# HGRN2 recurrence on one core: three short-column visits per head instead of four, and one projection operand re-read from DRAM

## The chip, the cores and the metric

The kernel runs on one core of one Trainium2 chip. The metric is device time in microseconds (us); the time of before is the median of three runs. One more execution was taken with the hardware profiler; its own time and span stand in the table further down.

## The reference, cut to what matters

A two-layer network over 1024 tokens of width 1024: layer 0 is sliding-window attention, layer 1 the HGRN2 recurrence; each is followed by a squared-ReLU MLP. The change touches layer 1 alone. There, eight heads of width 128 work in 16 chunks of 64 tokens:

```python
q, f, i, g = jnp.split(h @ w_in, 4, axis=-1)
...
def chunk_step(state, inp):
    qc, kc, vc, lc = inp                       # lc: log of the forget gate
    b = jnp.cumsum(lc, axis=2)
    o_inter = jnp.einsum('bhtd,bhde->bhte', qc * jnp.exp(b), state)
    diff = b[:, :, :, None, :] - b[:, :, None, :, :]
    decay = jnp.exp(jnp.where(causal[None, None, :, :, None], diff, -jnp.inf))
    scores = jnp.einsum('bhtd,bhtsd,bhsd->bhts', qc, decay, kc)
    o_intra = jnp.einsum('bhts,bhse->bhte', scores, vc)
    ...
```

`scores` is a 64 x 64 causal table per chunk whose entry (t, s) carries the product of all forget gates between s and t, for each of the 128 channels.

## The kernel before, in words

**The input projection.** `hgrn` runs eight heads. For each, `gates` calls `two` twice (q with g, then f with i). `two` multiplies by a seven-product scheme (Strassen-Winograd): the activations were prepared as seven operands `x[1]` to `x[7]`, each four tiles that are held as a rounded high part and a low part, in the buffer pool `a` (60 buffers of 256 KB). One product is 12 matmuls of 128x128 by 512 columns: high weights by high and by low activations, low weights (`wl`) by high activations. Each product goes to a PSUM bank of pool `p` and is read from there into a tile of pool `t` (18 buffers) by a copy on ScalarE or an addition on VectorE.

**The recurrence.** `recurrence` builds `scores` level by level. Level lg pairs neighbouring blocks of 2^lg tokens: the later block's queries meet the earlier block's keys. Between levels `double` multiplies the changed half of q and of k by the block products of the forget gates, so that after `double(H)` blocks of 2H tokens are joined. The score matmuls have 64 output rows each and are issued in pairs, one for each half of the array ("columns" in the code, `128*64` in the profile); all other matmuls use the whole array (`128*128`). A stretch of score matmuls between whole-array ones is called a *visit* here. Before, each head has four: diagonal (`own`) with level 0; levels 1 and 2; levels 3 and 4; level 5 with `cross`. `double(1)`, `double(4)` and `double(16)` write in place; `double(2)`, `double(8)` and `double(32)` write new tiles (their unchanged half is copied by ScalarE), because the two levels of a visit need the values before and after it. `late` lists every operand of a visit as an input of each of its matmuls, so no matmul of it starts before all are ready. `merge` puts a level's results into `scores` on VectorE (a predicated copy).

**The order.** All operations are recorded first, then a planner with a table of costs puts them in order on each engine and gives each tile its buffer; the kernel issues that order. `interleave` records the recurrence of head e-1 between the projection steps of head e, so the visits of a head stand among products of the next. Every operation is recorded by one helper, so all carry line 433 in the profile, and groups are told apart by tile names: `q<-t,t` in form `128*64` are the visits, `p<-a,wh` and `p<-a,wl` the projection. DMAs are all issued on SyncE's queue (SP), which takes them in order.

**Moving data to DRAM and back** is done by `put_by` (stores the two parts of an operand) and `take_back` (loads them into buffers of pool `a`).

Of the kernel before, what the change touches and what calls it, by code (L numbers as in the profile page):

```python
# [378 lines left out]
class Net:  # L379
# [1051 lines left out]
    def take_back(self, kept):  # L1431
# [2 lines left out]
            self.dma(v.bitcast(F32), k, 4 * P * TH)  # L1434
        return views

    def two_first(self, which, e, x):

        self.s.lead = LEAD
        w = [self.weight_split(self.raw(self.io["win"][which[0], e][:, c : c + TH])) for c in (0, TH)]  # L1440
        self.s.lead = 0
        main, own, y0 = self.psum(), self.psum(), self.t()
        self.product(main, w[0], x[1], True)
        self.copy(y0, main)
        self.product(own, w[1], x[2], True)
        self.tt("DVE", y0, own, y0, ALU.add)
        return main, y0

    def two(self, which, e, x, out, begun=None):

        w = self.strassen_weights(*(self.io["win"][i, e] for i in which), (1, 2) if begun else ())
        main, y0 = begun or (self.psum(), self.t())
        side, own = self.psum(), begun or self.psum()
        y1, z0, z1 = (self.t() for _ in range(3))
        out += [(y0, y1), (z0, z1)]
        if not begun:
            self.product(main, w[1], x[1], True)
            self.copy(y0, main)
        yield
        self.product(side, w[5], x[5], True)  # L1460
        self.copy(z1, side)
        yield
        self.product(main, w[6], x[6], False)
        self.copy(y1, main)
        yield
        if not begun:
            self.product(own, w[2], x[2], True)
            self.tt("DVE", y0, own, y0, ALU.add)
        yield
        self.product(main, w[7], x[7], False)  # L1470
        self.tt("DVE", z1, main, z1, ALU.add)
        yield
        self.product(side, w[3], x[3], False)
        self.tt("DVE", y1, side, y1, ALU.add)
        yield
        self.product(main, w[4], x[4], False)
        self.copy(z0, main)
        yield
# [31 lines left out]
    def recurrence(self, e, gates, totals, out):  # L1510

        nc = self.nc
        NC = NH * BPH
        chunk = lambda z, j: z[:, j * CH : j * CH + CH]
        scores = self.t(F32, (P, NC, CH))
        tots, tot = [self.t(tag="m") for _ in range(NH)], [g[1] for g in gates]
        qs, ks = ([g[i] for g in gates] for i in (0, 2))
        later = lambda z, H: z.rearrange("p (n a h) -> p n a h", a=2, h=H)[:, :, 1]
        at = 0

        def level(lg, part, qs, ks, late):
            H = 1 << lg
            for hf, (q, k) in enumerate(zip(qs, ks)):
                for c in range(BPH):
                    for b in range(2):
                        rows, j = slice(b * CH, b * CH + CH), 2 * c + b
                        self.mm(part[rows, hf * BPH + c], chunk(k, j), later(chunk(q, j), H), True, True, CH, 2.06, "columns", late)

        def merge(lg, part):
            H = 1 << lg  # L1530
            n = CH // (2 * H)
            mask = later(self.level_mask[lg], H).unsqueeze(1).to_broadcast([P, NC, n, H])
            target = scores.rearrange("p c (n a h) -> p c n a h", a=2, h=H)[:, :, :, 1]
            part = part.rearrange("p c (n h) -> p c n h", n=n)
            self.op("DVE", nc.vector.copy_predicated, [target], [mask, part], 70 + TH // 2 * 1.04, target, mask, part)

        def part_of(bank, i):
            return bank[:, i * TH // 2 : (i + 1) * TH // 2].rearrange("p (c t) -> p c t", c=NC)

        own = self.psum("q").rearrange("p (c t) -> p c t", c=NC)  # L1540
        part = part_of(self.psum("q"), 0)
        first = [self.t() for _ in range(NH)]
        for z, (q, f, k, g, v) in zip(first, gates):
            self.tt("any", z, q, f, ALU.mult)
        late = qs + ks + first
        for hf, (q, k) in enumerate(zip(qs, ks)):
            for c in range(BPH):
                for b in range(2):
                    rows, j = slice(b * CH, b * CH + CH), 2 * c + b
                    self.mm(own[rows, hf * BPH + c], chunk(k, j), chunk(q, j), True, True, CH, 2.06, "columns", late)  # L1550
        level(0, part, first, ks, late)
        self.tt("DVE", scores, own, self.diag.unsqueeze(1).to_broadcast([P, NC, CH]), ALU.mult)
        merge(0, part)
        qs = first
        yield
        at, tot, qs, ks = self.double(1, qs, ks, tot, tots, at)
        yield
        for lg in (1, 3, 5):
            bank = self.psum("q")
            at, tot, q2, k2 = self.double(1 << lg, qs, ks, tot, tots, at, True)  # L1560
            yield
            late = qs + ks + q2 + k2
            level(lg, part_of(bank, 0), qs, ks, late)
            if lg < LEVELS - 1:
                level(lg + 1, part_of(bank, 1), q2, k2, late)
            else:
                cross = self.psum("q")[:CH].rearrange("p (c t) -> p c t", c=NC)
                for hf, (q, k) in enumerate(zip(q2, k2)):
                    for c in range(BPH):
                        self.mm(cross[:, hf * BPH + c], chunk(k, 2 * c), chunk(q, 2 * c + 1), True, True, CH, 3.9, "columns", late)  # L1570
            merge(lg, part_of(bank, 0))
            qs, ks = q2, k2
            if lg < LEVELS - 1:
                merge(lg + 1, part_of(bank, 1))
                yield
                at, tot, qs, ks = self.double(2 << lg, qs, ks, tot, tots, at)
            yield
        weights = []
        for hf in range(NH):
            s, c = self.t(F32, (P, BPH, 2, CH)), slice(hf * BPH, hf * BPH + BPH)  # L1580
# [5 lines left out]
        at, tot, qs, ks = self.double(CH, qs, ks, tot, tots, at)  # L1586
# [4 lines left out]
        for hf, (q, k) in enumerate(zip(qs, ks)):  # L1591
# [13 lines left out]
            before = [state]  # L1605
# [26 lines left out]
        self.dma(z, kept, 4 * P * TH)  # L1632
        return z

    def double(self, H, qs, ks, tot, tots, at, apart=False):

        n, new, out = TH // (2 * H), [], ([], [])  # L1640
        for hf in range(NH):
            tv = tot[hf].rearrange("p (n a) -> p n a", a=2)
            for i, z in enumerate((qs[hf], ks[hf])):
                y = self.t() if apart else z
                zv, yv = (t.rearrange("p (n a h) -> p n a h", a=2, h=H) for t in (z, y))
                changed, factor = 1 - i, tv[:, :, i : i + 1].to_broadcast([P, n, H])
                if apart:
                    self.copy(yv[:, :, i].only(i), zv[:, :, i], TH // 2, ("ACT",), False)
                    self.tt("any", yv[:, :, changed].only(changed), zv[:, :, changed], factor, ALU.mult, TH // 2)
                else:  # L1650
                    self.tt("any", yv[:, :, changed], zv[:, :, changed], factor, ALU.mult, TH // 2)
                out[i].append(y)
            new.append(tots[hf][:, at : at + n].only(H))
            self.tt("DVE", new[hf], tv[:, :, 0], tv[:, :, 1], ALU.mult, n)
        return at + n, new, *out
# [124 lines left out]
    def hgrn(self, layer):  # L1780
        self.hgrn_constants()
        x, r = self.finish(layer, True), [self.a() for _ in range(NH)]
        begun = [self.two_first(which, 0, x) for which in ((0, 3), (1, 2))]
        self.rs.append(self.token_rstd(self.sum_squares([self.x[kt][1] for kt in range(KT)]), keep=True))
        for y, z in zip(r, self.rs):
            self.copy(y, self.spread(z))
        self.spill(1)
        y, totals, self.later = {k: [] for k in range(1, 8)}, [], []
        before = iter(())
        for e in range(KT):  # L1790
            got = []
            interleave(self.gates(e, x, self.rs, r, got, [None] * 2 if e else begun), before, 14, 13)
            before = self.recurrence(e, got, totals, y)
        run(before)
        first = self.mlp_first(layer)
        for _ in self.hgrn_out(y, totals):
            for _ in range(HK):
                next(first)
        run(first)
# [27 lines left out]
def run(pieces):  # L1827
    for _ in pieces:
        pass


def interleave(main, other, n_main, n_other):
    done = 0
    for k, _ in enumerate(main):
        while done * n_main < (k + 1) * n_other and next(other, run) is not run:
            done += 1
    run(other)
# [80 lines left out]
```

## Time and profile before

| | before |
|---|---|
| median of three runs | 2055.05 us (2054.32 to 2055.57) |
| the profiled execution's own time | 2054.78 us |
| its span, first to last instruction | 2053.0 us |
| mean granted TensorE clock | 0.999 of full speed |
| TensorE matmul busy / weight load busy | 2042.3 us (99%) / 1740.3 us (85%) |
| VectorE busy / ScalarE busy | 1853.4 us (90%) / 1289.1 us (63%) |
| DMA | 434.21 MB, mean 212 GB/s |

The time lies 1.8 us above the span. HGRN's heads occupy the span from about 950 to 1380 us; each takes about 53.7 us, the distance from one head's first visit to the next one's. Matmuls are pipelined, so the length of one (0.39 us for 512 columns) is not what it costs: that is read from the distance between starts.

### The profile page before, as it was taken

What the parts mean: (1) busy time and instruction counts of PE and PEld (TensorE: products, weight loads), DVE (VectorE), ACT (ScalarE), POOL (GpSimd) and SP (SyncE); (2) the same over time, 40 slices, a digit from 0 to 9 for tenths busy, and PEclk for the clock granted to TensorE, in tenths of its full rate; (3) what the DMA queues carried; (4) which work ended last, traced back from release to release, by engine and by line L of the source; (5) the groups of instructions that cost most, each with busy time, mean ns of one, the idle gap of its engine ahead of it and who ended that gap; (6) DMA issues with size and microseconds to landing.
All of it is one profiled execution on the core that took longest, in us unless ns stands there. A gap on an engine that the chain in (4) does not pass through costs nothing.

```text
span 2053.0 us, 36250 instructions
## 1 busy us (share of the span) xinstructions
PE 2042.3 (99%) x12300; PEld 1740.3 (85%) x12300; DVE 1853.4 (90%) x3751; ACT 1289.1 (63%) x2647; POOL 56.1 (3%) x120
## 2 busy tenths in 40 slices
PE   9999999999999999999999999999999999999998
PEld 8878888899998888888888888888889999888887
DVE  8899979899999979889988889999999899997985
ACT  7577976667675444666555555566777767544573
POOL 4030000000000000000000000000000000000000
PEclk9999999999999999999999999999999999999999
DMA  6212488688789977642333333689688888997812
GB/s 227 78 52 73 138 261 270 229 278 290 262 290 305 329 261 256 201 134 72 114 106 112 114 108 130 233 281 311 229 299 290 273 284 285 316 328 240 267 53 82
DMA packets 240841, 434.21 MB, mean 212 GB/s; under 512 B 27152, under 2 KB 32528, under 8 KB 240656
## 3 DMA queue, kind: packets, MB, share of 16 engines
q1 hardware_dynamic: 240512, 431.88, 63.0%
q8 instruction: 97, 1.59, 0.3%
q14 instruction: 88, 0.72, 0.1%
q10 hardware_dynamic: 144, 0.02, 0.0%
HBM read 335.85 MB, written 95.94 MB: 210 GB/s over the span
## 4 chain that ended last, share of the span: by engine, by line
PE 93%; DVE 6%; issue 1%; ACT 0%; DVEq 0%; ACTq 0%
PE p L433 50%; PE q L433 43%; DVE t L433 3%; DVE a L433 1%; DVE wl L433 1%; DVE m L433 1%; DVE sm L433 0%; ACT t L433 0%; ACT m L433 0%; ACT L433 0%; ACT wh L433 0%; ACT a L433 0%; DVEq L1892 0%; ACT sm L433 0%; DVEq L433 0%
## 5 line engine op out<-in xcount | busy, mean ns | idle before, releaser
L433 PE MATMUL p<-a,wh 128*128 128x512 f32 (+1 forms) x2832 | 781.1, 361 | 0.2
L433 PE MATMUL q<-a,wh 128*128 128x512 f32 x2020 | 625.9, 390 | 0.0
L433 PEld LDWEIGHTS p<-a,wh 128*128 128x128 f32 x2832 | 500.8, 189 | 79.0 <-ACT wh L433 1.0
L433 PE MATMUL p<-a,wl 128*128 128x512 f32 (+1 forms) x1416 | 504.3, 359 | 0.0
L433 PEld LDWEIGHTS q<-a,wh 128*128 128x128 f32 x2020 | 375.0, 188 | 74.2 <-DVE a L433 0.2
L433 PE MATMUL q<-a,wl 128*128 128x512 f32 x1008 | 391.8, 389 | 0.0
L433 ACT CAST wh<-m 128x512 fp32r<-128x512 f32 (+1 forms) x354 | 212.9, 606 | 208.2 <-PE q L433 100.0
L433 ACT CAST wh<-wr 128x512 fp32r<-128x512 f32 (+1 forms) x324 | 194.7, 604 | 179.6 <-PE p L433 115.1
L433 PEld LDWEIGHTS p<-a,wl 128*128 128x128 f32 x1416 | 266.1, 189 | 37.7
L433 DVE TENSOR_TENSOR wl<-m,wh 128x512 fp32r<-128x512 f32 x354 | 234.6, 667 | 38.9 <-ACT wh L433 32.9
L433 DVE TENSOR_TENSOR wl<-wr,wh 128x512 fp32r<-128x512 f32 (+1 forms) x324 | 214.0, 665 | 18.6 <-ACT wh L433 17.2
L433 DVE TENSOR_TENSOR t<-t,t 128x512 f32<-128x512 f32 (+3 forms) x376 | 217.5, 601 | 11.2 <-ACT t L433 8.3
L433 DVE TENSOR_TENSOR a<-t,a 128x512 fp32r<-128x512 f32 (+2 forms) x321 | 210.2, 674 | 18.0 <-ACT a L433 6.8
L433 ACT ACTIVATE t<-t 128x512 f32<-128x512 f32 x288 | 179.6, 631 | 69.1 <-DVE t L433 64.1
L433 PEld LDWEIGHTS q<-a,wl 128*128 128x128 f32 x1008 | 189.3, 188 | 39.0 <-DVE wl L433 0.2
L433 ACT CAST a<-t 128x512 fp32r<-128x512 f32 (+1 forms) x241 | 142.3, 607 | 22.9 <-DVE t L433 8.7
L433 DVE TENSOR_TENSOR t<-t,p 128x256 f32<-128x256 f32 x288 | 115.6, 414 | 13.6 <-PE p L433 10.1
L433 PE MATMUL p<-wh,a 128*128 128x512 f32 x384 | 125.7, 397 | 0.3 <-DVE a L433 0.3
L433 DVE TENSOR_TENSOR m<-wr,wr 128x512 f32<-128x512 f32 (+1 forms) x184 | 119.1, 649 | 0.4
L433 ACT COPY t<-q 128x512 f32<-128x512 f32 (+2 forms) x174 | 95.2, 556 | 24.3 <-PE q L433 19.0
L433 DVE TENSOR_TENSOR a<-a,a 128x512 fp32r<-128x512 f32 (+2 forms) x151 | 100.8, 679 | 8.8 <-PE q L433 3.4
L433 PEld LDWEIGHTS q<-t,t 128*64 128x64 f32 (+1 forms) x2160 | 95.8, 144 | 13.5 <-issue 7.3
(131 smaller groups left out, 2492.2 us busy)
## 6 DMA issues: line engine op xcount, KB each, us to landing
t<-d SPq DMA_DIRECT2D x592, 256.0 KB, 4.5
d<-t SPq DMA_DIRECT2D x290, 256.0 KB, 3.2
wr<-in_down SPq DMA_DIRECT2D x224, 256.0 KB, 4.2
wr<-in_up SPq DMA_DIRECT2D x172, 256.0 KB, 4.2
a<-d SPq DMA_DIRECT2D x94, 256.0 KB, 4.4
wr<-in_win SPq DMA_DIRECT2D x68, 256.0 KB, 2.8
wr<-in_wqkv SPq DMA_DIRECT2D x48, 256.0 KB, 3.0
d<-a SPq DMA_DIRECT2D x48, 256.0 KB, 3.5
```

The source lines that it names most:

```text
L433: fn(*[place(a) for a in args], **{k: place(v) for k, v in kw.items()})
```

## The change

`double(1)` now writes new tiles as well (`apart` is a function that gives the tile; all calls pass `self.t`), so that the values before and after it both exist. The first visit is moved behind `double(1)` and `double(2)` and takes the diagonal and levels 0, 1 and 2 at once, in three PSUM banks. Visits two and three are the old three and four. Apart from that, the four tiles of operand `x[5]` are stored to DRAM after they are made (eight stores); head 0 still uses them from where they are, and heads 1 to 7 load them again for each of their two products (14 times eight loads of 256 KB).

```diff
+    def fetched(self, operands):
+        return [self.take_back(z) if isinstance(z, list) else z for z in operands]
...
-        self.product(side, w[5], x[5], True)
+        self.product(side, w[5], self.fetched(x[5]), True)
...
-        own = self.psum("q").rearrange("p (c t) -> p c t", c=NC)
-        part = part_of(self.psum("q"), 0)
         first = [self.t() for _ in range(NH)]
         for z, (q, f, k, g, v) in zip(first, gates):
             self.tt("any", z, q, f, ALU.mult)
-        late = qs + ks + first
+        yield
+        at, tot, q1, k1 = self.double(1, first, ks, tot, tots, at, self.t)
+        yield
+        at, tot, q2, k2 = self.double(2, q1, k1, tot, tots, at, self.t)
+        yield
+        own, low, two = (self.psum("q") for _ in range(3))
+        own = own.rearrange("p (c t) -> p c t", c=NC)
+        late = qs + ks + first + q1 + k1 + q2 + k2
...
-        level(0, part, first, ks, late)
+        level(0, part_of(low, 0), first, ks, late)
+        level(1, part_of(low, 1), q1, k1, late)
+        level(2, part_of(two, 0), q2, k2, late)
         self.tt("DVE", scores, own, self.diag.unsqueeze(1).to_broadcast([P, NC, CH]), ALU.mult)
-        merge(0, part)
-        qs = first
+        merge(0, part_of(low, 0))
+        merge(1, part_of(low, 1))
+        merge(2, part_of(two, 0))
+        qs, ks = q2, k2
         yield
-        at, tot, qs, ks = self.double(1, qs, ks, tot, tots, at)
+        at, tot, qs, ks = self.double(4, qs, ks, tot, tots, at)
         yield
-        for lg in (1, 3, 5):
+        for lg in (3, 5):
...
-                y = self.t() if apart else z
+                y = apart() if apart else z
...
+        streamed = {**x, **{name: [self.put_by(z) for z in x[name]] for name in (5,)}}
...
-            interleave(self.gates(e, x, self.rs, r, got, [None] * 2 if e else begun), before, 14, 13)
+            interleave(self.gates(e, streamed if e else x, self.rs, r, got, [None] * 2 if e else begun), before, 14, 13)
```

How this moves instructions, first on TensorE's queue, at the visits of the fourth head (e = 3). The rows are the instructions in the order in which they are issued; `x8` is a run of alike ones, and each row of score matmuls stands for both halves of the array. Before:

```order
5308 L433 MATMUL p_13862<-a_11084,wl_13679 128x512
5309 L433 MATMUL q_13912<-t_13281,t_13765 64x64 x8
5310 L433 MATMUL q_13912<-t_13394,t_13841 64x64 x8
5311 L433 MATMUL q_13937<-t_13846,t_13765 64x32 x8
5312 L433 MATMUL q_13937<-t_13839,t_13841 64x32 x8
5313 L433 MATMUL p_13960<-a_11477,wh_13728 128x512
...
5348 L433 MATMUL p_14026<-a_11123,wl_13763 128x512
5349 L433 MATMUL q_14056<-t_13846,t_13765 64x32 x8
5350 L433 MATMUL q_14056<-t_13839,t_13841 64x32 x8
5351 L433 MATMUL q_14056<-t_13971,t_13975 64x32 x8
5352 L433 MATMUL q_14056<-t_13984,t_13979 64x32 x8
```

The same place now:

```order
5344 L433 MATMUL p_14150<-a_11131,wl_13915 128x512
5345 L433 MATMUL q_14185<-t_13411,t_13917 64x64 x8
5346 L433 MATMUL q_14185<-t_13478,t_13996 64x64 x8
5347 L433 MATMUL q_14205<-t_14017,t_13917 64x32 x8
5348 L433 MATMUL q_14205<-t_14027,t_13996 64x32 x8
5349 L433 MATMUL q_14205<-t_14075,t_13923 64x32 x8
5350 L433 MATMUL q_14205<-t_14056,t_14081 64x32 x8
5351 L433 MATMUL q_14245<-t_14091,t_14100 64x32 x8
5352 L433 MATMUL q_14245<-t_14112,t_14137 64x32 x8
```

Before, 36 whole-array matmuls (rows 5313 to 5348) stood between the first visit and the second; now the two are one, and its last rows stand where the second visit's last rows stood. The 45 whole-array matmuls between the last transposes ahead of it (row 5299) and the merged visit run without a break.

On ScalarE's queue, the copies of `double`'s unchanged halves for the same head (`t_...<-t_...`; the shape tells the doubling, 128x256 being `double(1)` and 128x128x2 `double(2)`), and the copies `t<-p` that free a projection bank. Before:

```order
1276 L433 CAST wh_13910<-m_13643 128x512
1277 L433 COPY t_13918<-p_13862 128x512
1278 L433 ACTIVATE t_13866<-q_13874,c_11446 128x128 x2
1279 L433 COPY t_13971<-t_13846 128x128x2
1280 L433 COPY t_13975<-t_13765 128x128x2
1281 L433 COPY t_13979<-t_13841 128x128x2
1282 L433 COPY t_13984<-t_13839 128x128x2
```

Now:

```order
1290 L433 COPY t_14075<-t_14017 128x256
1291 L433 COPY t_14081<-t_13996 128x256
1292 L433 COPY t_14088<-p_14020 128x512
1293 L433 COPY t_14091<-t_14075 128x128x2
1294 L433 COPY t_14100<-t_13923 128x128x2
1295 L433 CAST wh_14105<-m_13800 128x512
1296 L433 COPY t_14112<-t_14056 128x128x2
1297 L433 CAST wh_14117<-wr_13530 128x512
1298 L433 COPY t_14126<-p_14068 128x512
1299 L433 COPY t_14137<-t_14081 128x128x2
```

There are four more copies per head (two of them stand earlier on the queue), and copies that free a projection bank now stand between those that the merged visit needs.

On SP's queue, a re-load of `x[5]` (`a<-d`) and the weight loads (`wr<-in_win`) of the same projection, now:

```order
895 L433 DMA d_13747<-t_13683 128x512
896 L433 DMA a_13761<-d_11484 128x512
897 L433 DMA a_13770<-d_11500 128x512
...
902 L433 DMA a_13814<-d_11589 128x512
903 L433 DMA a_13832<-d_11598 128x512
904 L433 DMA wr_13845<-in_win 128x512
```

Before, no loads into `a` stood there. The weight loads now stand behind the eight re-loads.

More of the change, by code (lines that the diff above doesn't have):

```diff
@@ L1550, in recurrence @@
                     self.mm(own[rows, hf * BPH + c], chunk(k, j), chunk(q, j), True, True, CH, 2.06, "columns", late)
-        level(0, part, first, ks, late)
+        level(0, part_of(low, 0), first, ks, late)
+        level(1, part_of(low, 1), q1, k1, late)
+        level(2, part_of(two, 0), q2, k2, late)
         self.tt("DVE", scores, own, self.diag.unsqueeze(1).to_broadcast([P, NC, CH]), ALU.mult)
-        merge(0, part)
-        qs = first
+        merge(0, part_of(low, 0))
+        merge(1, part_of(low, 1))
+        merge(2, part_of(two, 0))
+        qs, ks = q2, k2
         yield
-        at, tot, qs, ks = self.double(1, qs, ks, tot, tots, at)
+        at, tot, qs, ks = self.double(4, qs, ks, tot, tots, at)
         yield
-        for lg in (1, 3, 5):
+        for lg in (3, 5):
             bank = self.psum("q")
-            at, tot, q2, k2 = self.double(1 << lg, qs, ks, tot, tots, at, True)
+            at, tot, q2, k2 = self.double(1 << lg, qs, ks, tot, tots, at, self.t)
             yield
@@ L1633, in back, with double @@
         return z
-    def double(self, H, qs, ks, tot, tots, at, apart=False):
+    def double(self, H, qs, ks, tot, tots, at, apart=None):
         n, new, out = TH // (2 * H), [], ([], [])
```

## The prediction

> **What bounds the kernel now.** I read the page first: busy time by engine, the granted clock by slice and the chain that ended last.
>
> ```profile
> span 2053.0 us, 36250 instructions
> PE 2042.3 (99%) x12300; PEld 1740.3 (85%) x12300; DVE 1853.4 (90%) x3751; ACT 1289.1 (63%) x2647; POOL 56.1 (3%) x120
> PEclk9999999999999999999999999999999999999999
> PE 93%; DVE 6%; issue 1%; ACT 0%; DVEq 0%; ACTq 0%
> ```
>
> TensorE is busy throughout at full granted clock and holds 93% of the chain. A busy figure of pipelined matmuls doesn't prove a bound, so the second view is the stage that the change touches: the waits of TensorE between 950 and 1340 us, and busy time head by head (one row for the fourth head, two for the last two; columns: stretch, its length, then busy us and instructions of PE, PEld, DVE, ACT, POOL, then clock, DMA share, GB/s).
>
> ```profile
> PE q L433 <- ACT t L433: 0.2, 1, 0.2
> ```
>
> ```profile
> 1112.00:1165.00 53.00, 53.00 (x466) 44.81 (x465) 46.91 (x104) 29.08 (x62) 0.56 (x2) 1.00 0.32 110
> 1273.00:1326.00 53.00, 53.00 (x466) 44.83 (x466) 49.43 (x109) 30.53 (x65) 0.61 (x2) 1.00 0.55 184
> 1326.00:1380.00 54.00, 53.98 (x502) 46.16 (x501) 52.21 (x124) 35.27 (x76) 0.62 (x2) 1.00 0.85 299
> ```
>
> TensorE waits once in 390 us, for 0.2 us. VectorE has 6.1 us to spare in the fourth head, 3.6 in the seventh, 1.8 in the last. So what shortens TensorE's queue in this stage shortens the run, as long as the other engines keep delivering in time.
>
> **What a visit costs.** The third view is TensorE's timeline round the fourth head's second visit (start, length, form, count), and two narrow cuts inside that visit (rows with x60 and x10).
>
> ```profile
> 1133.81 0.39 PE L433 MATMUL p<-a,wl 128*128 128x512 f32 x1
> 1134.13 2.06 PE L433 MATMUL q<-t,t 128*64 128x32 f32 x64
> 1136.12 0.73 PE L433 MATMUL p<-a,wh 128*128 128x512 f32 x2
> 1136.68 0.40 PE L433 MATMUL p<-a,wl 128*128 128x512 f32 x1
> 1136.92 0.62 PE L433 MATMUL p<-a,wh 128*128 128x512 f32 x2
> ...
> 1143.73 0.61 PE L433 MATMUL p<-a,wh 128*128 128x512 f32 x2
> ...
> 1144.50 2.06 PE L433 MATMUL q<-t,t 128*64 128x32 f32 x64
> ```
>
> ```profile
> 1134.27 1.92 PE L433 MATMUL q<-t,t 128*64 128x32 f32 x60
> 1135.72 0.46 PE L433 MATMUL q<-t,t 128*64 128x32 f32 x10
> ```
>
> A whole-array matmul takes a step of 0.227 us: 30 of them between the starts 1136.92 and 1143.73, 6.81 us. A pair of score matmuls takes 0.058 us: 50 records, 25 pairs, between 1134.27 and 1135.72. From 1133.81 to 1136.68 are 2.87 us, in which three whole-array steps (0.68) and 32 pairs (1.86) stand. The remaining 0.33 us is what the visit costs beyond its work: 0.09 on entering (1134.13 - 1133.81 - 0.227), 0.13 inside, at its ends, and 0.11 in the first two whole-array matmuls after it (0.56 where two steps are 0.45). No idle time is shown; it hides in the distance between starts.
>
> **The change part by part.**
>
> *One visit less per head.* The merged visit does the same 64 pairs without the break: 8 x 0.33 = 2.7 us less. All of it lies on the path, since TensorE doesn't wait here. Lower bound: if only the entry goes, 8 x 0.09 = 0.7 us. I take 2.7, because going from one group of pairs to the next inside a visit is an ordinary step in these rows.
>
> The Trainium skill's page "TensorEngine Tiling (Array Packing)", section "Key Properties", says that changing the tiling mode drains TensorE. Its page "TensorE: Matmul & The Clock Gate", section "Step-by-step: what each phase is for", gives the drain as some 128 cycles. By that, an estimate for two drains per visit at 2.4 GHz is 0.11 us, and 0.9 us for eight visits. The measured 0.33 us per visit decides for the size; that switching costs, the rows and the page agree.
>
> *What the merged visit waits for.* It needs the tiles of `double(1)` and `double(2)`, which the old second visit already needed, and its last rows stand in the queue where that visit's stood. When those were ready shows on VectorE and ScalarE in the fourth head, and for the tightest case in the last head, whose old second visit began at 1348.89:
>
> ```profile
> 1127.20 1.42 DVE L433 TENSOR_TENSOR t<-t,m 128x256 f32<-128x256 f32 x4
> 1126.31 1.49 ACT L433 COPY t<-t 128x256 f32<-128x256 f32 x4 [1.04 <-DVE t L433]
> ...
> 1346.95 1.42 DVE L433 TENSOR_TENSOR t<-t,m 128x256 f32<-128x256 f32 x4
> 1348.89 2.06 PE L433 MATMUL q<-t,t 128*64 128x32 f32 x64
> ```
>
> In the fourth head the last input is done at 1128.62, 5.5 us ahead of the visit at 1134.13. Moreover `double(1)` need no longer wait for the first visit to have read what it overwrites. In the last head it is done at 1348.37, 0.5 us ahead, and TensorE didn't wait. I take 0 for this wait, with a bound of 0.5 us in each of the last three heads.
>
> *Four more copies per head, on ScalarE, and the same multiplications on VectorE.*
>
> ```profile
> L433 ACT COPY t<-t x112: 394/407/457, 965.6 to 1320.1; 128x256 f32<-128x256 f32 x84, 64x256 f32<-64x256 f32 x28
> L433 DVE TENSOR_TENSOR t<-t,m 128x256 f32<-128x256 f32 x24 | 8.5, 416 | 0.0
> L433 DVE TENSOR_TENSOR t<-t,t 128x256 f32<-128x256 f32 x4 | 1.4, 416 | 0.0
> ```
>
> 4 x 0.41 = 1.6 us per head on an engine with 18.7 idle even in the last stretch (54 - 35.27): nothing on the path. Were ScalarE full, it would be 8 x 1.6 = 13 us. VectorE's multiplications cost 0.416 us whether the result goes to a new tile or in place (the first of the two groups holds both), so 0; the diagonal and the merges only move together.
>
> *The fifth operand from DRAM.* 8 stores once, and 14 times 8 loads of 256 KB. The nearest row of the DMA issues, with the median time to landing last, and the first visits of the third and the fourth head:
>
> ```profile
> a<-d SPq DMA_DIRECT2D x94, 256.0 KB, 4.4
> ```
>
> ```profile
> 1070.06 2.06 PE L433 MATMUL q<-t,t 128*64 128x64 f32 x64
> 1123.76 2.06 PE L433 MATMUL q<-t,t 128*64 128x64 f32 x64
> ```
>
> A load lands 4.4 us after its issue. A head lasts 53.7 us (1123.76 - 1070.06). Per head 16 loads are 4.2 MB in 53.7 us, 78 GB/s on top of 110 to 184; the kernel sustains 299 in the stretch from 1326. At 299 GB/s eight loads move in 7.0 us. Their buffers come free when the product before has been done, half a head (27 us) ahead of use, so 11.4 us of queue and landing leave some 15 us. On SP's queue the weight loads of the same projection stand behind them and are delayed with them by at most these 7 us, which the same margin covers. Head 1's first loads must also wait for the new stores, which are issued ahead of head 0's products, most of a head before their use. I take 0; if the cover were gone at one place, eight loads late by their own 7.0 us would make 2052.4 + 7.0 = 2059.4.
>
> *Buffers.* Over the merged visit 15 of the 18 `t` tiles are alive on the recurrence's side (q, k, `first`, q1, k1, q2, k2, two each, and `scores`); at the old second visit it was 9. Three are left for the evacuations of the 45 matmuls ahead of it, which are three products and a part of a fourth. It just fits; this is the weak place.
>
> **The sum.** 2054.78 (the profiled execution) - 2.7 = 2052.1; that execution lies 0.3 us below the median of the runs, so the median to expect is 2052.4 us, 0.13% less. A difference of 0.2%, 4.1 us, is about what a measurement of this kernel can tell from no change.
>
> **The rivals.**
>
> *VectorE is the bound in the last three heads.* The Trainium skill's page "Perfetto Trace Analysis", section "Identifying the Most-Contended Engine", says to judge TensorE by its weight-load busy share and to take the fullest engine as the one that limits. For: VectorE at 52.21 of 54 us in the last stretch, weight loads at 46.16. Against: TensorE's steps show no wait. Then only the first five heads gain, 5 x 0.33 = 1.7 us: 2053.4. By the page's rule for the whole stage the time would not move: 2055.05.
>
> *A late evacuation: slower.* With three free `t` tiles, a copy `t<-p` on ScalarE's queue may have to wait for a tile that only the merged visit frees. Behind it on that queue stand copies that the merged visit itself needs, and the bank that it should empty is wanted by the product after the visit. TensorE then waits for the copy once the tile is free:
>
> ```profile
> L433 ACT COPY t<-p 128x512 f32<-128x512 f32 x8 | 4.6, 579 | 0.0
> ```
>
> 0.58 us and a hand-over of about 0.2 us, 0.8 us in each of the seven heads that overlap with a projection: 5.6 - 2.7 = 2.9 us slower, 2058.0. Two such copies in a row make 11.2 - 2.7, 2063.6. The sign turns at 0.39 us per head (2.7/7), and at 0.97 it passes 0.2%. Against it: the tightest wait before (0.5 us to spare) cost nothing.
>
> *The change doesn't do what it says.* Only the entry is saved, 0.7 us: 2054.3.
>
> *More is gained.* If the shorter chain also takes away waits elsewhere, over 4.1 us in all are needed, 1.4 beyond the visits. TensorE's waits from 950 to 1340 us are 0.2 us, so there is little to win: 2050.9.
>
> **How the numbers follow.** Forecast 0.66 (2051.2 to 2053.4, the rounding of 0.33 and the spread of runs), VectorE 0.09, only the entry 0.03, late evacuation 0.14 (0.04 up to 2058.0, 0.10 beyond 0.2%), late re-loads at one place 0.02, more gained 0.06. Within 0.2% are 0.66 + 0.09 + 0.03 + 0.04 = 0.82; slower 0.12, faster 0.06. The slower 0.12 are 0.10 + 0.02. The range from 2051.2 to 2058.0 holds the first three cases and the near part of the fourth, 0.82.
>
> **What would show it.** Right: 24 visits instead of 32; the merged one lasts 2.06 + 1.86 = 3.9 us by the timeline's length; its first matmul starts 0.32 us after the start of the last whole-array one; the time from one first visit to the next falls from 53.7 to 53.4 us; TensorE's waits stay under 1 us in the stage. Wrong: a wait of TensorE for ScalarE or VectorE ahead of a merged visit or in the product after it (late evacuation), a wait for `a<-d` or for `wh`, `wl` ahead of the fifth product (streaming), or a stretch in which VectorE has no idle time while TensorE has.

## The result, and the profile after

The changed kernel takes 2051.54 us (median of 22 runs, 2051.06 to 2052.51) against 2054.95 us before on the same chip (22 runs, 2054.22 to 2055.57): a ratio of 0.9984, 95% interval 0.9978 to 0.9990. That is 3.4 us less where 2.7 were forecast, at the lower end of the range (2051.2 to 2058.0). The gain is 0.17%; the interval leaves out no change, so the runs tell apart less than the 0.2% that the prediction took for their limit. The profiled execution took 2051.76 us, 3.0 less than that of before.

The page of after, the rows that stand in the prediction for before:

```profile
span 2050.0 us, 36535 instructions
PE 2040.0 (100%) x12300; PEld 1740.6 (85%) x12300; DVE 1852.9 (90%) x3751; ACT 1299.2 (63%) x2679; POOL 57.5 (3%) x120
PEclk9999999999999999999999999999999999999999
PE 96%; DVE 3%; issue 0%; ACT 0%; DMA 0%; SPq 0%; DVEq 0%; ACTq 0%
```

TensorE is as full as before and holds still more of the chain; ScalarE has 32 instructions more. The same stretches of the recurrence, busy time by engine (columns as in the prediction):

```profile
1112.00:1165.00 53.00, 53.00 (x467) 45.07 (x467) 47.05 (x104) 30.77 (x67) 0.61 (x2) 1.00 0.55 189
1273.00:1326.00 53.00, 53.00 (x466) 44.86 (x465) 49.45 (x113) 31.96 (x71) 0.56 (x2) 1.00 0.71 244
1326.00:1380.00 54.00, 54.00 (x498) 46.59 (x497) 51.13 (x117) 36.27 (x80) 0.61 (x2) 1.00 0.82 287
```

No wait of TensorE is listed from 950 to 1340 us. The DMA share (the mean busy share of the core's DMA engines) in the fourth head went from 0.32 to 0.55 and the rate from 110 to 189 GB/s: 79 more, where the prediction worked out 78. TensorE's timeline at the merged visit of the third head (first row: its beginning) and of the fourth:

```profile
1077.11 0.39 PE L433 MATMUL q<-t,t 128*64 128x64 f32 x6
...
1130.13 0.39 PE L433 MATMUL p<-a,wl 128*128 128x512 f32 x1
1130.45 3.92 PE L433 MATMUL q<-t,t 128*64 128x64 f32 x128
1134.31 0.73 PE L433 MATMUL p<-a,wh 128*128 128x512 f32 x2
1134.88 0.40 PE L433 MATMUL p<-a,wl 128*128 128x512 f32 x1
```

64 pairs run without a break, 3.92 us by the timeline's length. The entry is as before, 0.32 from start to start, so the visit waited for nothing. One head's first visit follows the other's by 53.34 us (1130.45 - 1077.11); it was 53.70 (1123.76 - 1070.06): 0.36 less. The whole stage has 24 visits where it had 32.

### The profile page after: what moved, and what is told of

Its sections match the earlier page's. It is cut to its first block, busy times and chain, and to the rows that moved or that the text cites. A ratio compares the mean times of both kernels' runs of the same rounds, so it can differ in the third digit from the quotient of the medians.

```text
span 2050.0 us, 36535 instructions
## 1 busy us (share of the span) xinstructions
PE 2040.0 (100%) x12300; PEld 1740.6 (85%) x12300; DVE 1852.9 (90%) x3751; ACT 1299.2 (63%) x2679; POOL 57.5 (3%) x120
## 4 chain that ended last, share of the span: by engine, by line
PE 96%; DVE 3%; issue 0%; ACT 0%; DMA 0%; SPq 0%; DVEq 0%; ACTq 0%
PE p L433 52%; PE q L433 44%; DVE a L433 1%; DVE t L433 1%; DVE m L433 0%; DVE sm L433 0%; DVE wl L433 0%; DMA a<-in_x 0%; ACT m L433 0%; SPq L433 0%; ACT t L433 0%; ACT a L433 0%; ACT wh L433 0%; DVEq L1905 0%; DVEq L433 0%
```

## The experiments

Each run was compared with runs of the kernel before on the same chip; *less* and *more* below are against those.

### The two halves of the change, each alone

Before with streaming only, four visits a head:

```diff
+    def fetched(self, operands):
+        return [self.take_back(z) if isinstance(z, list) else z for z in operands]
...
-        self.product(side, w[5], x[5], True)
+        self.product(side, w[5], self.fetched(x[5]), True)
...
+        streamed = {**x, **{name: [self.put_by(z) for z in x[name]] for name in (5,)}}
```

> The streaming of x[5] alone, with the four visits of before. Theory (the gain is the cost of eight visits, 0.33 us each, and the streaming is hidden): same time as before within 0.5 us, TensorE's waits between 940 and 1340 us under 1 us, 32 visits. Rival (the streaming gives a part of the gain, since eight buffers of pool a come free and the planner orders head 0 otherwise): 0.5 to 1 us faster than before, and the two short losses of before at 942.5 and 1002.9 us gone. Second rival (the streaming costs something that the merging pays for): slower than before by 1 us or more.

Measured: 2055.05 us against 2054.72, ratio 1.0001 (0.9992 to 1.0010). TensorE's waits from 950 to 1340 us are 0.2 us, as before. Streaming is hidden, and by itself it gives nothing.

The merge only:

```diff
-        streamed = {**x, **{name: [self.put_by(z) for z in x[name]] for name in (5,)}}
+        streamed = {**x, **{name: [self.put_by(z) for z in x[name]] for name in ()}}
```

> The merged visit alone, x[5] kept where it is. Theory: 2.7 us faster than before from the eight visits, and up to 0.7 us more if the two short losses of before at 942.5 and 1002.9 us go with the new order: a ratio of 0.9984 to 0.9987, the same as with the streaming. Rival (without the eight freed buffers the recurrence's longer-lived tiles hold up the projection): within 1 us of before or slower, with TensorE waiting for ScalarE or VectorE.

Measured: 2052.64 us, 2.1 less, ratio 0.9990 (0.9981 to 0.9999). So the merge carries the gain. The two halves don't add up to the whole (-2.1 and +0.3 against -3.4); the last experiments come back to this.

### The price of a visit

Three small whole-array matmuls (128 columns, into an unused part of a bank) are put into each merged visit, ahead of levels 0, 1 and 2, so that it falls into four. The control has the same three ahead of the visit.

```diff
...
+        for lg, part, q, k in ((0, part_of(low, 0), first, ks), (1, part_of(low, 1), q1, k1), (2, part_of(two, 0), q2, k2)):
+            self.mm(spare, self.ident, self.ident, True, True, P, 1.0, "whole", late)
+            level(lg, part, q, k, late)
```

and in the control, ahead of the first `level`:

```diff
...
+        for _ in range(3):
+            self.mm(spare, self.ident, self.ident, True, True, P, 1.0, "whole", late)
```

> The changed kernel with the merged visit broken in three places by one whole-array matmul of 128 columns (identity by identity, into an unused part of a bank): 24 more breaks over eight heads, the output is the same. Theory (a visit's overhead of 0.33 us is paid at each break): 24 x (0.33 + 0.11 for the matmul itself) = 10.6 us slower than the changed kernel, 8.0 us slower than the kernel with the same 24 matmuls ahead of the visit. Rival (the 0.11 us after a visit belongs to the change from plain to rounded fp32 operands and not to the change of the array's shape, so a plain matmul in the break doesn't pay it): 24 x 0.22 = 5.3 us slower than the one with the matmuls ahead. Second rival (only the entry of 0.09 us is paid): 2.2 us.

> The changed kernel with the same three whole-array matmuls of 128 columns per head, all ahead of the merged visit instead of inside it. Every theory: 24 x 0.11 = 2.7 us slower than the changed kernel (a step of 0.11 us each), so close to before; it is the control for the breaks.

Measured: 2064.59 us with the breaks (9.9 more, ratio 1.0048, 1.0036 to 1.0061) and 2056.43 without (1.7 more, 1.0009, 1.0000 to 1.0018). The difference is 8.16 us for 24 more visits, **0.34 us each**, where the theory had 0.33. Both rivals are out: a switch between plain and rounded operands as the cause of 0.11 of it would have given 5.3 us, the entry alone 2.2. TensorE's timeline with the breaks, fourth head:

```profile
1135.14 1.15 PE L433 MATMUL q<-t,t 128*64 128x64 f32 x32
1136.22 0.49 PE L433 MATMUL q<-c 128*128 128x128 f32 x2
1136.64 1.12 PE L433 MATMUL q<-t,t 128*64 128x32 f32 x32
1137.69 0.49 PE L433 MATMUL q<-c 128*128 128x128 f32 x2
1138.11 1.12 PE L433 MATMUL q<-t,t 128*64 128x32 f32 x32
```

and of the control:

```profile
1132.17 0.40 PE L433 MATMUL p<-a,wl 128*128 128x512 f32 x1
1132.40 0.83 PE L433 MATMUL q<-c 128*128 128x128 f32 x6
1133.16 3.92 PE L433 MATMUL q<-t,t 128*64 128x64 f32 x128
```

From 1136.64 to 1138.11 are 1.47 us; 16 pairs at 0.058 are 0.93, and two records of the small matmul, at 0.11 each as the control shows (1133.16 - 1132.40 is 0.76, less 0.09 on entering, by six), are 0.22. What remains is 0.32. The control also shows why its own time was forecast too low: three small matmuls are six records, 0.67 us a head and not half of that. Over eight heads this makes 5.4 us where 2.7 were forecast; the control lies 4.9 above the changed kernel.

### A second merge

Levels 3, 4, 5 and `cross` of a head in one visit too: 16 visits. That needs more buffers, so `x[6]` is streamed as well.

```diff
-        self.product(main, w[6], x[6], False)
+        self.product(main, w[6], self.fetched(x[6]), False)
...
-        for lg in (3, 5):
...
+        at, tot, q3, k3 = self.double(8, qs, ks, tot, tots, at, self.t)
...
+        at, tot, q4, k4 = self.double(16, q3, k3, tot, tots, at, self.t)
...
+        at, tot, q5, k5 = self.double(32, q4, k4, tot, tots, at, self.a)
...
+        level(3, part_of(low, 0), qs, ks, late)
+        level(4, part_of(low, 1), q3, k3, late)
+        level(5, part_of(two, 0), q4, k4, late)
...
-        streamed = {**x, **{name: [self.put_by(z) for z in x[name]] for name in (5,)}}
+        streamed = {**x, **{name: [self.put_by(z) for z in x[name]] for name in (5, 6)}}
```

> The second merge: levels 3, 4, 5 and the cross-chunk products of a head in one visit too (16 visits in all where the changed kernel has 24), with the input projection's sixth operand, x[6], streamed beside x[5]; twelve tiles are moved to the score matmuls' corner per head ahead of the visit, two of its pairs in the a pool. Theory (a visit costs TensorE 0.33 us, all else is hidden): 8 visits fewer x 0.33 us = 2.7 us below the changed kernel, about 2048.9 us. Rival 'covers run out' (t tiles held longer, or streaming of two operands late): TensorE waits appear in the stage and the time is at or above the changed kernel's 2051.5 us. Rival 'most of the change's gain was the two short losses of the first two heads, not the visits': under 1 us below the changed kernel.

The control, the changed kernel with both operands streamed and nothing merged further:

```diff
-        self.product(main, w[6], x[6], False)
+        self.product(main, w[6], self.fetched(x[6]), False)
...
-        streamed = {**x, **{name: [self.put_by(z) for z in x[name]] for name in (5,)}}
+        streamed = {**x, **{name: [self.put_by(z) for z in x[name]] for name in (5, 6)}}
```

> The changed kernel with x[6] streamed as well as x[5], nothing merged further (25 visits: one of the seventh head's is split by the order). Theory (loads are hidden, a visit costs 0.33 us): +0.3 us for the one split visit, between 2051.3 and 2052.3 us. Rival 'streaming itself gives time back' (x[5] streamed left 1.1 us between the merge alone and the whole change): about 1 us below the changed kernel, 2050.5 us.

Measured: 2051.57 us with the second merge (3.3 less, ratio 0.9984, 0.9975 to 0.9993), 2053.79 for the control (1.1 less, 0.9994, 0.9986 to 1.0003). The second merge gains 2.2 us over its control, most of the 9 x 0.33 = 3.0; but against the changed kernel nothing is gained, since the control lies 2.2 us above that. Neither the 2048.9 forecast for the one nor the 2051.3 to 2052.3 for the other came. Where it went is seen just ahead of the first head's visits, from 930 to 946 us. Busy time there in the changed kernel:

```profile
930.00:946.00 16.00, 16.00 (x72) 13.21 (x71) 15.93 (x27) 9.98 (x18) 0.00 (x0) 1.00 0.15 47
```

and in the control (its second row is the fourth head, of use further down):

```profile
930.00:946.00 16.00, 14.91 (x63) 10.91 (x62) 15.72 (x27) 8.82 (x16) 0.00 (x0) 1.00 0.45 152
...
1112.00:1165.00 53.00, 53.00 (x466) 45.03 (x465) 46.99 (x105) 30.37 (x68) 0.61 (x2) 1.00 0.73 257
```

TensorE's waits in that stretch, in the control's timeline (in brackets the idle time ahead of the row and what ended it):

```profile
942.85 0.50 PE L433 MATMUL p<-a,wh 128*128 128x512 f32 x1 [0.47 <-DVE a L433]
944.06 0.50 PE L433 MATMUL p<-a,wh 128*128 128x512 f32 x1 [0.24 <-DVE a L433]
...
945.86 0.49 PE L433 MATMUL p<-a,wl 128*128 128x512 f32 x1 [0.38 <-DVE wl L433]
```

VectorE prepares the operands `a` and the weights' low parts (`wl`) there, and it is the one that TensorE waits for. The control gets 9 matmuls fewer done (63 against 72), which at 0.227 us each are 2.0 of the 2.2 us. But VectorE is full in both (15.93 and 15.72 of 16 us), and the changed kernel waits for nothing. So a full VectorE alone doesn't cost; I take it that the order decides which operand comes too late. The 16-visit kernel has the same losses there.

To leave that place alone, the second merge was tried with the same edit of the levels and `x[5]` alone streamed (18 visits, `for name in (5,)`):

> Two visits a head as in the run before, but with x[5] alone streamed, as in the changed kernel: up to the first head's visits the order of instructions is the changed kernel's, so the stretch from 942 to 946 us, in which streaming x[6] cost 1.7 us, is not touched. 18 visits stand in the order (two heads have one more, split by the order) where the changed kernel has 24. Theory: no loss at 942 to 946 us and 6 x 0.33 = 2.0 us below the changed kernel, about 2049.5 us. Rival 'the next merge uses up a cover' (the a pool holds two more tiles per head without a second streamed operand, so loads or evacuations come late): TensorE waits within the heads, at or above the changed kernel's 2051.5 us. Rival 'the loss at 942 us belongs to the second merge and not to the streaming': 1.7 us stand there again, about 2051.2 us.

Measured: 2052.18 us (2.6 less, ratio 0.9987, 0.9977 to 0.9996), where 2049.5 was forecast. In the middle of the stage the visit is won; the third and the fourth head begin their first visits at

```profile
1077.25 0.28 PE L433 MATMUL q<-t,t 128*64 128x64 f32 x2
...
1130.24 0.34 PE L433 MATMUL q<-t,t 128*64 128x64 f32 x4
```

52.99 us apart, 0.35 less than the 53.34 above. The stretch ahead of the first head's visits is free of loss, too. But other short waits have come: one within the heads, at 1002.54, where before waited too (the list of TensorE's waits from 950 to 1340: total, number, longest), one after the last visit (the timeline), one of 0.5 us for ScalarE at 1371, and one of 0.4 us behind the heads:

```profile
PE q L433 <- ACT t L433: 0.4, 1, 0.4
```

```profile
1361.07 0.66 PE L433 MATMUL q<-c,a 128*128 128x128 f32 x4 [0.36 <-DVE a L433]
```

### How far streaming can go, and the pool that was called weak

Three operands streamed:

```diff
-        self.product(main, w[6], x[6], False)
+        self.product(main, w[6], self.fetched(x[6]), False)
...
-        self.product(main, w[7], x[7], False)
+        self.product(main, w[7], self.fetched(x[7]), False)
...
-        streamed = {**x, **{name: [self.put_by(z) for z in x[name]] for name in (5,)}}
+        streamed = {**x, **{name: [self.put_by(z) for z in x[name]] for name in (5, 6, 7)}}
```

> The changed kernel with x[5], x[6] and x[7] streamed: the order of instructions now breaks visits to feed the projection, and 65 visits stand in it where there were 24, while the arithmetic is the same. Theory (each visit 0.33 us, nothing else changes): 41 x 0.33 = 13.5 us above the changed kernel, about 2065 us. Rival 'the loads become the bound': TensorE waits for loads show in the stage, and the time lies well above 2067 us. Rival 'only the entry of a visit is paid' (0.09 us): 41 x 0.09 = 3.7 us, about 2055 us.

Measured: 2083.21 us (2079.72 to 2085.90), 28.3 more, ratio 1.0136 (1.0123 to 1.0150). The theory's 2065 is far off; the time lies where the rival of the loads put it. Its busy time in the fourth head and ahead of the eighth:

```profile
1112.00:1165.00 53.00, 51.90 (x445) 42.57 (x445) 46.45 (x102) 28.18 (x64) 0.61 (x2) 1.00 0.91 326
1300.00:1326.00 26.00, 25.03 (x186) 18.42 (x184) 21.74 (x54) 11.81 (x27) 0.61 (x2) 0.76 0.97 339
```

and the longest of its waits from 950 to 1340 us:

```profile
PE p L433 <- DVE t L433: 2.3, 3, 1.1
PE p L433 <- ACT t L433: 1.1, 2, 0.8
PE p L433 <- DVE wl L433: 1.0, 1, 1.0
PE p L433 <- DMA a<-d: 0.9, 2, 0.5
```

The DMA share is 0.91 in the fourth head, where it was 0.55 with one operand and 0.73 with two; TensorE waits, and 41 visits more stand in the order. The granted clock of 0.76 is a mean over 26 us. Within them it stands at half:

```profile
1316.00:1324.00 8.00, 8.00 (x90) 6.84 (x90) 4.87 (x11) 3.25 (x7) 0.31 (x1) 0.50 1.03 357
```

TensorE's two waits for loads end just ahead of that, at 1311.59 and 1312.89; that order in time is all that the trace shows of a cause. The four executions of this kernel took 2079.72, 2082.04, 2084.38 and 2085.90 us at mean clocks of 0.999, 0.998, 0.997 and 0.995. The profiled one is the last, so some 6 us of its time go with the clock.

Its span is 34.1 us longer than the changed kernel's (2084.1 against 2050.0). The visits explain 13.5 of them by 41 x 0.33, and the clock some 6. The waits from 950 to 1390 us are 6.4 in all, of which only 0.9 name a load. The other 8 or so I did not separate, so that the loads became the bound is not shown. It answers the question in this far: one and two operands run without TensorE waiting for a load in the heads, three do not.

The changed kernel with 17 `t` buffers for 18:

```diff
-BUFS = {"a": 60, "t": 18, "m": 6, "sm": 8, "wr": 6, "wh": 5, "wl": 5, "p": 4, "q": 4}
+BUFS = {"a": 60, "t": 17, "m": 6, "sm": 8, "wr": 6, "wh": 5, "wl": 5, "p": 4, "q": 4}
```

> The changed kernel with 17 t tiles instead of 18, which is the pool that the prediction called the weak place; the order has 26 visits in place of 24. Theory (the pool has just enough; two visits more): +0.7 us, 2052 to 2053 us. Rival 'late evacuation' (with 15 of the t tiles held over the merged visit, only two are left for the products' evacuations): TensorE waits for t tiles ahead of the merged visits, of the order of 0.5 us a head, 4 us more, above 2055 us.

Measured: 2052.65 us (2.2 less, ratio 0.9990, 0.9981 to 0.9998). No wait of TensorE is listed from 950 to 1340 us; two of its 26 visits are splits that the order makes. Outside the heads it waits 0.4 us for `wh` ahead of them and 0.9 us for a load behind them, so the 1.1 us that it lies above the changed kernel are not all the splits. Late evacuation, which would have put it above 2055, did not come at 17 either. That the pool has room to spare isn't shown, since with 17 the order splits two visits.

### The order alone

The planner's estimate for ScalarE's copies out of SBUF is shifted by a few ns. The instructions and the number of visits stay at those of the changed kernel (first two) and of the merge alone (third); only their order moves.

```diff
-        ways = {"ACT": self.call(self.nc.scalar.copy, out, in_) + ((52 if psum else 94) + n * 0.834 + more,)}
+        ways = {"ACT": self.call(self.nc.scalar.copy, out, in_) + ((52 if psum else 84) + n * 0.834 + more,)}
```

The second has 99 in that place, the third 84 in the merge alone.

> The changed kernel with one number of the planner altered: it reckons ACT's copies out of SBUF 10 ns shorter. The instructions are the same and so are the 24 visits; only the order in which the engines' instructions stand shifts a little. Theory (what is left beside 0.33 us a visit is short losses at the edges of the stage that any shift of the order rearranges): it differs from the changed kernel's 2051.5 us by up to 1.5 us either way, with no loss inside the heads. Rival 'the 1.1 us between the merge alone and the whole change is what streaming x[5] gives': with streaming and merge both in it, it stays at 2051.5 us within 0.4 us.

> As the run before, with ACT's copies out of SBUF reckoned 5 ns longer. Theory: within 1.5 us of the changed kernel's 2051.5 us, and not by the same amount as the run before. Rival (streaming gives the 1.1 us): 2051.5 us within 0.4 us.

> The merge alone, without streaming, with ACT's copies out of SBUF reckoned 10 ns shorter by the planner; 24 visits. Theory: within 1.5 us of the merge alone (2052.6 us), and it may lie under the changed kernel. Rival (streaming gives the 1.1 us): 2052.6 us within 0.4 us, above both runs before it.

Measured: 2054.02 us (ratio 0.9995, 0.9986 to 1.0004), 2051.72 (0.9984, 0.9975 to 0.9993) and 2052.77 (0.9989, 0.9980 to 0.9998), beside 2054.92 before. Two kernels with the same work and the same 24 visits differ by 2.3 us, and the first lies 2.5 above the changed kernel, where 1.5 was allowed for. The second and the third stayed within 0.4 us of the kernels that they vary, as the rival had it for them; the first did not. The first one's busy time at the place seen before:

```profile
930.00:946.00 16.00, 15.44 (x71) 12.21 (x70) 16.00 (x27) 8.10 (x15) 0.00 (x0) 1.00 0.06 21
```

VectorE is full for all 16 us, and TensorE's waits from 930 to 947 are

```profile
PE p L433 <- DVE wl L433: 0.4, 1, 0.4
PE p L433 <- DVE a L433: 0.2, 1, 0.2
```

From 950 to 1340 it has none. So the 1.1 us between the merge alone and the whole change needn't be what streaming gives: a shift of the order moves more than that. The five kernels with 24 visits and no added matmuls gain 0.9, 2.1, 2.1, 3.2 and 3.4 us, 2.3 on average, where eight visits are worth 2.6. Taking 0.33 us off before's time for each visit that a kernel has fewer than 32, the kernels with 16 to 26 visits, those with added matmuls left out, lie between 0.8 us below that line (the changed one) and 2.0 above it (18 visits). None is clearly below the changed kernel.

## Why the prediction was right, point by point

**The bound.** Right: TensorE is the bound in the heads, and what its queue loses there the time loses.

**The price of a visit.** Right: 0.33 forecast, 0.34 by the added breaks, 0.32 by their timeline, 0.35 in the distance of heads at the second merge. The 0.11 us estimated from the drain in the Trainium skill's page "TensorE: Matmul & The Clock Gate", section "Step-by-step: what each phase is for", is a third of it; the measurement decides. That only the entry is saved is refuted by the breaks (2.2 us against 8.16).

**The copies, the multiplications, the operand from DRAM.** Right, all at nothing. ScalarE's busy time grew from 1289.1 to 1299.2 us, VectorE's went from 1853.4 to 1852.9. In after, the group of ScalarE's copies from 950 to 1340 us (shortest, median and longest in ns) and two rows of the DMA issues (median time to landing last) are

```profile
L433 ACT COPY t<-t x143: 393/408/487, 962.6 to 1339.9; 128x256 f32<-128x256 f32 x115, 64x256 f32<-64x256 f32 x28
```

```profile
a<-d SPq DMA_DIRECT2D x206, 256.0 KB, 4.5
wr<-in_win SPq DMA_DIRECT2D x68, 256.0 KB, 4.0
```

In the window there are 143 of these copies where there were 112, at the same 0.41 us. The row of loads into `a` holds the 94 of before and 112 re-loads; they land 4.5 us after issue (4.4 forecast); the weight loads behind them take 4.0 us, which was 2.8 before, as foreseen of that queue. TensorE waits for none of either in the heads.

**The wait for the visit's inputs.** Right at 0, with less to spare than worked out. The last multiplication and copy ahead of the fourth head's visit, and the last copy ahead of the eighth's, which begins at 1345.61:

```profile
1126.97 0.42 DVE L433 TENSOR_TENSOR t<-t,m 128x256 f32<-128x256 f32 x1
1126.34 0.47 ACT L433 COPY t<-t 128x256 f32<-128x256 f32 x1
...
1344.72 0.44 ACT L433 COPY t<-t 128x256 f32<-128x256 f32 x1
1345.61 3.92 PE L433 MATMUL q<-t,t 128*64 128x64 f32 x128
```

3.1 us to spare in the fourth head (1130.45 - 1127.39), where 5.5 were taken from the old order, and 0.45 in the eighth, about the 0.5 of the prediction.

**The rivals.** Late evacuation showed in the heads of no run but the one with three operands streamed. There products wait 1.1 us for ScalarE and 2.3 us for VectorE to take an earlier product out of its bank; what held these up I did not follow. The hand-over of about 0.2 us in that rival's price stands in no row. In that run TensorE goes on 0.05 us after such a copy's end (1244.60 + 0.58 to 1245.23).

VectorE didn't bind in the last two heads: it has 3.6 and 2.9 us of idle time in the stretches quoted above. By the rule of the Trainium skill's page "Perfetto Trace Analysis", section "Identifying the Most-Contended Engine" (the fullest engine limits, TensorE taken by its weight loads), the time would not have moved at all; here the trace doesn't agree. Yet in some of the kernels TensorE waits for VectorE in a place that the prediction didn't look at, the 16 us ahead of the first head's visits.

**The step that was too small.** "TensorE's waits from 950 to 1340 us are 0.2 us, so there is little to win". The window began 8 us too late, and idle time shows only a part of what is lost. TensorE's timeline of before, at two places:

```profile
942.48 1.52 PE L433 MATMUL p<-a,wh 128*128 128x512 f32 x4
943.84 0.40 PE L433 MATMUL p<-a,wl 128*128 128x512 f32 x1
...
1002.26 0.40 PE L433 MATMUL p<-a,wl 128*128 128x512 f32 x1
1002.88 0.71 PE L433 MATMUL q<-t,t 128*128 128x128 f32 x4 [0.22 <-ACT t L433]
```

and of after:

```profile
942.50 0.39 PE L433 MATMUL p<-a,wl 128*128 128x512 f32 x1
942.73 0.62 PE L433 MATMUL p<-a,wh 128*128 128x512 f32 x2
943.18 0.39 PE L433 MATMUL p<-a,wl 128*128 128x512 f32 x1
943.41 0.62 PE L433 MATMUL p<-a,wh 128*128 128x512 f32 x2
943.86 0.39 PE L433 MATMUL p<-a,wl 128*128 128x512 f32 x1
...
1001.68 0.40 PE L433 MATMUL p<-a,wl 128*128 128x512 f32 x1
1001.91 1.16 PE L433 MATMUL q<-t,t 128*128 128x128 f32 x8
```

Before, four steps take 1.36 us from 942.48 (0.91 at 0.227 each) and one takes 0.62 from 1002.26; after, the steps are 0.23 at both places. That is 0.45 + 0.39 = 0.8 us beside the 2.6 to 2.7 of the visits. Together they are 3.4 to 3.5, as the medians have it; the two profiled spans differ by 3.0, and the executions of one kernel by more than the 0.4 us between (2054.22 to 2055.57 before). The loss at 942 is there with streaming alone (four steps take 1.34 us) and with the merge alone (0.41 us of idle time). It is gone in the changed kernel, and with the 10 ns shift, both halves in it, it is back. The one at 1002 stands again (0.21 us of idle time) in the changed kernel with the 5 ns shift. Since the same work in a slightly other order also has such losses, I put the 0.8 us down to the order and don't call it an effect of either half. The prediction priced the change at one order, and had no term for what another order does: in these runs from 0.8 us less to 2.0 more, against a change worth 2.7. So the price of a visit was right by its reason, but that the time fell within 2051.2 to 2053.4, which got 0.66, was in part luck: the order with the 10 ns shift gave 2054.02.

## What to carry to other kernels

Price a switch of the array's shape by the distance between starts on both sides of it, not by idle time, and test the price by adding switches to a copy that has the same extra matmuls without them. Where a planner writes the order, run the change also with a planner's number shifted by a trifle: that tells how much of a gain of a few us belongs to the change. And look for waits ahead of the stage as well as in it: with two operands streamed, the 16 us there cost 2.0 us, nearly what the change is worth.

## What the runs showed that I had not expected

A small whole-array fp32 matmul of 128 columns stands as two records of 0.11 us (three of them took 0.67 us). With three operands streamed the granted clock stood at 0.50 from 1316 to 1324 us in the profiled execution, while the DMA engines were busy throughout (a share of 1.03 in that view); it was 1.00 in the stretches quoted of the other kernels. The executions of that kernel spread by 6 us, the longer the lower their mean clock, where the others spread by about 1. What caused the lower clock isn't settled.
